# Running sums of a feed-forward's down product: kept in SBUF between loads and stores, or added to in memory by accumulating transfers

## The chip, the cores and the metric

The kernel runs on one core of a Trainium2 chip. The metric is the device time of one execution in microseconds (us), as the median of three runs; the runs lie between 1864.41 and 1867.26 us.

## The reference, cut to what matters

One layer on 256 tokens of width 2048: a mixer (dilated attention and a gated linear attention), a layer norm, a convolved feed-forward of inner width 5632, and a second layer norm. Everything is float32. The change lies in the last lines.

```
ALPHA = (2 * DEPTH) ** 0.25
...
def _conv_ffn(x, w_gate, w_up, conv_w, conv_b, w_down):
    g = x @ w_gate
    ...
    return (jax.nn.silu(gc) * (x @ w_up)) @ w_down
...
        x = _layernorm(ALPHA * x + mix, ln1_g[i], ln1_b[i])
        ffn = _conv_ffn(x, ffn_w_gate[i], ffn_w_up[i], ffn_conv_w[i], ffn_conv_b[i], ffn_w_down[i])
        x = _layernorm(ALPHA * x + ffn, ln2_g[i], ln2_b[i])
```

So the second norm is taken of `ALPHA * x + ffn`, where x is the output of the first norm; `ALPHA * x` is called the residual below.

## The kernel before

**Products.** A float32 product is made of three fast ones: each operand is split into a high part (ScalarE, a rounding copy, tile `whi` for weights) and a low part (VectorE, source minus high part, tile `wlo`), both at lines 145 and 146 (`split`). TensorE then multiplies high by high, high by low and low by high. All weights stream in as pieces of 128x1024 numbers, `raw` or `quarter`, on SyncE's queue. So for nearly every piece of weight there is one ScalarE and one VectorE instruction of over 1 us, then some 5 us of matmuls for four pieces.

**Feed-forward.** The 44 tiles of the inner width are cut into six parts (`FSPLIT = (8, 8, 8, 8, 8, 4)`). In each part the gate and up products of 8 tiles (4 in the last part) are made, convolved and gated into `h`; then `down_group` multiplies `h` with the rows of w_down that belong to the part. The down product of a part has 256 x 2048 sums: four column blocks n of 512, each for two token halves t, so eight blocks of 128x512, in the two PSUM banks of `mbank`. They are to be added up over the six parts.

**Order.** In part p > 0 steps of several kinds are mixed by a string, `MIX`: `u` a step of a Strassen-like unit (`seven`, products named fguA, fguB, fguD, fguE) that makes four tiles of gate and up at once, `t` a gate or up tile made directly (fg, fu), `A` a transposing and gating step of the unit of the part before (matmuls `pt`), `d` a step of the down product of the part before (`wd_t`), `B` an `A` of the last unit. For eight tiles it is `uAtAuAtAdutdudtdutdudtutdtd`, so two `d` finish one n. The framework's scheduler then sets the order of each engine's queue; each engine runs its own queue strictly in that order. A boundary between two parts means below: the last `d` of one string and the first `u A t A u A t A` of the next.

**Running sums before.** Tile `ACC[t][n]` is a block in device memory. In part 0 `more` copies the finished PSUM bank to SBUF with ScalarE (line 1118) and stores it ("spill") from GpSimd's queue. In parts 1 to 4 `ahead` has fetched the block into SBUF one n earlier (tile `af`, GpSimd's queue), `more` adds the PSUM bank to it with VectorE (line 1116) and spills it to a new block. The last four blocks of part 4 (n of 2 and 3) stay in SBUF; its first four are spilled and reloaded from ScalarE's queue into `acc` (line 1213), and part 5 adds its PSUM banks to all eight in SBUF with VectorE.

**Residual before.** x lies transposed in memory, `X1F`, eight blocks `x1f`. In the down product of part 0, after the first `d` of each n, eight float32 matmuls of blocks of x1f with `weighted` (ALPHA times the identity, made by VectorE at the start) add the turned residual to the PSUM banks (line 1137, tile names `wd_t<-weighted,x1f`; the compiler makes two records of each).

**Sums of x.** The units need sums of blocks of x: `sums_get(j)` fetches blocks j and j+4 of X1F into tiles `x1p`, `sums_part(j)` makes the sums (`comb`). These are called by `pump` between the steps of part 0.

**Buffers.** Most tiles of 128x512 (`blk`) in this stage share eight buffers: af, wd, x1p, x1f, and s, u, c of the units. A new tile takes the buffer of one that is done with, and the first instruction that writes it waits for the last reader of the old one, which for a spilled tile is the DMA.

## Time and profile before

| what | value |
| --- | --- |
| median of three runs | 1867.16 us (1864.41 to 1867.26) |
| profiled execution: span, first to last instruction | 1866.8 us |
| what lies around the span of the profiled execution | no time of its own is printed; the median of the runs is 0.4 us above the span |
| TensorE (PE) busy | 1819.1 us, 97% |
| VectorE (DVE) busy | 1442.1 us, 77% |
| ScalarE (ACT) busy | 1084.1 us, 58% |
| GpSimd (POOL) busy | 238.7 us, 13% |
| mean granted TensorE clock | 0.991 |
| feed-forward, from the end of the first norm | 1130 to 1867 us of the span |

An engine's busy time is the sum of its instructions; PEld is the loading of weights into TensorE, beside its matmuls. In a row of the timeline the square bracket tells how long the engine sat idle before the instruction and what released it. The boundaries between parts lie at about 1349, 1481, 1611 and 1740 us of the span (into parts 2, 3, 4 and 5).

### The profile page before, as it was taken

What the parts mean: (1) busy time and instruction counts of PE and PEld (TensorE: products, weight loads), DVE (VectorE), ACT (ScalarE), POOL (GpSimd) and SP (SyncE); (2) the same over time, 40 slices, a digit from 0 to 9 for tenths busy, and PEclk for the clock granted to TensorE, in tenths of its full rate; (3) what the DMA queues carried; (4) which work ended last, traced back from release to release, by engine and by line L of the source; (5) the groups of instructions that cost most, each with busy time, mean ns of one, the idle gap of its engine ahead of it and who ended that gap; (6) DMA issues with size and microseconds to landing.
All of it is one profiled execution on the core that took longest, in us unless ns stands there. A gap on an engine that the chain in (4) does not pass through costs nothing.

```text
span 1866.8 us, 25420 instructions
## 1 busy us (share of the span) xinstructions
PE 1819.1 (97%) x8974; PEld 1523.3 (82%) x8974; DVE 1442.1 (77%) x1715; ACT 1084.1 (58%) x1400; POOL 238.7 (13%) x361
## 2 busy tenths in 40 slices
PE   8999999999999999999999999999999999999896
PEld 6887887888887888888788868888888888888785
DVE  6978899788697978865856556886696877877878
ACT  5656586565666667646645345655565546655553
POOL 0121111111111111211300001011111110110211
PEclk9999999999999999999999999999999999999998
DMA  8898888987979798897965538569679779778782
GB/s 298 280 343 229 279 273 265 337 241 242 339 207 342 204 325 268 267 358 247 329 206 191 169 118 298 182 193 322 214 217 352 221 215 347 206 247 328 191 271 91
DMA packets 145420, 478.54 MB, mean 256 GB/s; under 512 B 17649, under 2 KB 27916, under 8 KB 145292
## 3 DMA queue, kind: packets, MB, share of 16 engines
q1 hardware_dynamic: 96764, 345.09, 51.6%
q0 software_dynamic: 34416, 118.62, 25.6%
q10 hardware_dynamic: 14112, 13.21, 2.2%
q8 instruction: 70, 1.15, 0.2%
q14 instruction: 58, 0.48, 0.1%
HBM read 382.41 MB, written 32.67 MB: 222 GB/s over the span
## 4 chain that ended last, share of the span: by engine, by line
PE 72%; issue 11%; DVE 7%; DMA 6%; ACT 2%; POOL 1%; SPq 0%; ACTq 0%; DVEq 0%; POOLq 0%
PE qk L236 9%; PE qk L238 5%; PE wd_t L273 4%; PE wd_t L272 4%; PE wd_t L274 4%; DMA raw<-in_wp 3%; DVE wlo L146 3%; PE gqk L236 3%; PE fguE L343 3%; PE fu L236 3%; PE fg L236 3%; PE fguA L343 2%; PE mD L343 2%; PE mA L343 2%; PE mE L343 2%
## 5 line engine op out<-in xcount | busy, mean ns | idle before, releaser
L146 DVE TENSOR_TENSOR wlo<-quarter,whi 128x1024 fp32r<-128x1024 f32 x484 | 578.8, 1219 | 217.1 <-issue 58.7
L145 ACT ACTIVATE whi<-quarter 128x1024 fp32r<-128x1024 f32 x484 | 504.8, 1057 | 301.0 <-DVE quarter L356 59.8
L145 ACT ACTIVATE whi<-raw 128x1024 fp32r<-128x1024 f32 (+1 forms) x346 | 358.5, 1051 | 246.8 <-DMA raw<-in_wp 121.6
L146 DVE TENSOR_TENSOR wlo<-raw,whi 128x1024 fp32r<-128x1024 f32 (+1 forms) x346 | 413.2, 1213 | 99.1 <-ACT whi L145 50.3
L236 PE MATMUL qk<-x,whi 128*128 128x512 f32 x768 | 189.2, 397 | 0.0
L359 POOL DMA_DIRECT2D quarter<-quarter x120 | 106.6, 912 | 616.4 <-DVE quarter L356 150.9
L236 PEld LDWEIGHTS qk<-x,whi 128*128 128x128 f32 x768 | 142.9, 188 | 30.2 <-issue 1.4
L356 DVE TENSOR_TENSOR quarter<-quarter,quarter 128x1024 f32<-128x1024 f32 x120 | 142.5, 1216 | 1.7 <-DMA quarter<-in_wp 1.5
L273 PE MATMUL wd_t<-wlo,h 128*128 128x512 f32 x352 | 137.4, 391 | 0.6 <-DVE wlo L146 0.6
L272 PE MATMUL wd_t<-whi,h 128*128 128x512 f32 x352 | 137.4, 393 | 0.2 <-ACT whi L145 0.2
L274 PE MATMUL wd_t<-whi,h 128*128 128x512 f32 x352 | 136.6, 389 | 0.0
L238 PEld LDWEIGHTS qk<-x,wlo 128*128 128x128 f32 x768 | 98.5, 191 | 3.7
L238 PE MATMUL qk<-x,wlo 128*128 128x256 f32 x768 | 99.6, 283 | 0.0
L236 PE MATMUL fu<-x,whi 128*128 128x512 f32 x368 | 87.9, 391 | 0.3 <-DVE gc L1045 0.3
L236 PE MATMUL fg<-x,whi 128*128 128x512 f32 x352 | 84.1, 391 | 0.0
L236 PEld LDWEIGHTS fu<-x,whi 128*128 128x128 f32 x368 | 68.3, 188 | 14.8 <-PE pt L1086 1.1
L274 PEld LDWEIGHTS wd_t<-whi,h 128*128 128x128 f32 x352 | 66.1, 188 | 14.2 <-DVE h L146 0.3
L273 PEld LDWEIGHTS wd_t<-wlo,h 128*128 128x128 f32 x352 | 66.2, 188 | 13.6 <-DVE wlo L146 0.9
L272 PEld LDWEIGHTS wd_t<-whi,h 128*128 128x128 f32 x352 | 65.9, 188 | 13.8 <-ACT whi L145 0.6
L236 PEld LDWEIGHTS fg<-x,whi 128*128 128x128 f32 x352 | 65.5, 188 | 13.3
L236 PE MATMUL gqk<-x,whi 128*128 128x512 f32 x256 | 65.3, 407 | 3.9 <-ACT whi L145 3.9
L236 PEld LDWEIGHTS gqk<-x,whi 128*128 128x128 f32 x256 | 49.5, 198 | 17.3 <-ACT whi L145 7.4
(375 smaller groups left out, 3185.2 us busy)
## 6 DMA issues: line engine op xcount, KB each, us to landing
raw<-in_wp SPq DMA_DIRECT2D x342, 512.0 KB, 6.0
quarter<-in_wp SPq DMA_DIRECT2D x304, 512.0 KB, 7.2
quarter<-quarter POOLq DMA_DIRECT2D x120, 512.0 KB, 10.1
af<-acc POOLq DMA_DIRECT2D x32, 256.0 KB, 6.9
acc<-af POOLq DMA_DIRECT2D x28, 256.0 KB, 5.7
sp<-c POOLq DMA_DIRECT2D x14, 256.0 KB, 9.5
bias<-bvd ACTq DMA_DIRECT2D x32, 96.0 KB, 6.6
v<-vs ACTq DMA_DIRECT2D x24, 128.0 KB, 4.6
```

The lines of the kernel that those rows point to most:

```text
L145: newest[:] = [nc.scalar.activation(hi, src, AF.Copy)]
L146: nc.vector.tensor_tensor(lo, src, hi.bitcast(F32), op=ALU.subtract)
L236: nc.tensor.matmul(ps, parts(kc)[0], opnd(kc), start=(kc == 0), stop=False)
L238: nc.tensor.matmul(ps[:, S:], parts(kc)[1], opnd(kc)[:, :S], start=False, stop=(kc == nk - 1))
L272: nc.tensor.matmul(ps, xh, hi, start=first, stop=False)
L273: nc.tensor.matmul(ps, xh, lo, start=False, stop=False)
L274: nc.tensor.matmul(ps, xl, hi, start=False, stop=last)
L343: nc.tensor.matmul(ps, a(kc)[which], w[:, k * 512 : (k + 1) * 512], start=(first and w is hi and which == 0 and kc == 0), stop=(w is lo an ...
L356: tt(a, a, b, op=ALU.add)
L359: nc.gpsimd.dma_start(a, b, accum_op=ALU.add)
```

## The change

ACC becomes four tiles in memory, one for each n, of 128x2x512. Their first value is the residual: `sums_part(j)`, which already has blocks j and j+4 of x in SBUF, also turns them with plain transposes on TensorE (`pr`, four for a block), ScalarE copies each full bank times ALPHA to a tile `res`, and GpSimd's queue stores it. Then in parts 0 to 4 (in part 4 only for n of 0 and 1) ScalarE copies each finished PSUM bank to a tile `wd`, and a DMA with `accum_op=add` on GpSimd's queue adds it to the block in memory. The fetches of x1f and of af and VectorE's adds of these parts are gone, but for n of 2 and 3 in part 4, which are fetched and added as before. `weighted` and its matmuls are gone.

```
--- before.py
+++ after.py
@@ -419,8 +419,6 @@
 
     ident = cpool.tile([P, P], F32, name="ident")
     make_identity(nc, ident)
-    weighted = cpool.tile([P, P], F32, name="weighted")
-    nc.vector.tensor_scalar(weighted, ident, ALPHA, None, op0=ALU.mult)
     prm = cpool.tile([P, NPAR], F32, name="prm")
     nc.gpsimd.dma_start(prm, par)
     pc = lambda c: prm[:, c : c + 1]
@@ -1093,7 +1091,7 @@
         return seven("fgu", X1, comb1, AT["fgu", f0], keep_it), [turned(f) for f in range(f0, f0 + 4)]
 
     F = [[None] * 4 for _ in range(2)]
-    ACC = [[None] * 4 for _ in range(2)]
+    ACC = [dpool.tile([P, 2, 512], F32, name=f"acc_{n}") for n in range(4)]
 
     def down_group(part, nf, hs):
 
@@ -1103,25 +1101,20 @@
 
         def ahead(n):
 
-            for t in range(2):
-                if part:
-                    st[n, t] = fetch("af", ACC[t][n])
-                else:
-                    st[n, t] = fetch("x1f", X1F[2 * n + t])
+            if part == len(FSPLIT) - 2 and n > 1:
+                for t in range(2):
+                    F[t][n] = fetch("af", ACC[n][:, t])
 
         def more(n, pss):
             for t in range(2):
-                a = F[t][n] if last else st[n, t] if part else blk("wd0")
-                if part:
-                    nc.vector.tensor_tensor(a, a, pss[t], op=ALU.add)
+                if F[t][n] is not None:
+                    nc.vector.tensor_tensor(F[t][n], F[t][n], pss[t], op=ALU.add)
                 else:
+                    a = blk("wd")
                     nc.scalar.activation(a, pss[t], AF.Copy)
+                    nc.gpsimd.dma_start(ACC[n][:, t], a, accum_op=ALU.add)
                 if last:
-                    nc.vector.bn_stats(stats[t][:, n, :], a)
-                elif part == len(FSPLIT) - 2 and n > 1:
-                    F[t][n] = a
-                else:
-                    ACC[t][n] = spill("acc", a)
+                    nc.vector.bn_stats(stats[t][:, n, :], F[t][n])
 
         def step(n, k0):
             def g():
@@ -1131,20 +1124,11 @@
                     if n < 3:
                         ahead(n + 1)
                 chunk_step(st["ps"], hk, nf, at, k0)
-                if not k0 and not part:
-                    for t in range(2):
-                        for k in range(4):
-                            nc.tensor.matmul(
-                                st["ps"][t][:, k * P : (k + 1) * P],
-                                st[n, k // 2][:, (k % 2) * S + t * P : (k % 2) * S + (t + 1) * P],
-                                weighted, start=False, stop=False
-                            )
                 if k0 + 4 == nf:
                     more(n, st["ps"])
             return g
 
         if not last:
-            ahead(0)
             return [step(n, k0) for n in range(4) for k0 in range(0, nf, 4)]
         for n in range(0, 4, 2):
             at = [AT["wd", part] + 2 * (n + i) for i in range(2)]
@@ -1176,7 +1160,19 @@
         return f
 
     def sums_part(j):
-        return lambda: part1(j)
+        def f():
+            part1(j)
+            for h in (j, j + 4):
+                pt = bank("pr")
+                for t in range(2):
+                    for k in range(2):
+                        c = t * S + k * P
+                        nc.tensor.transpose(pt[:, c : c + P], XF[h, t][:, k], ident)
+                a = blk("res")
+                nc.scalar.activation(a, pt, AF.Copy, scale=ALPHA)
+                c = (h % 2) * S
+                nc.gpsimd.dma_start(ACC[h // 2][:, :, c : c + S], a.rearrange("p (t c) -> p t c", t=2))
+        return f
 
     idle = lambda: None
     sums = [sums_get(0), idle, sums_get(1), sums_part(0), idle, sums_get(2), sums_part(1), idle, sums_get(3), sums_part(2), idle, sums_part(3)]
@@ -1210,7 +1206,7 @@
             for n in range(2):
                 for t in range(2):
                     F[t][n] = acc[:, 2 * t + n]
-                    nc.scalar.dma_start(F[t][n], ACC[t][n])
+                    nc.scalar.dma_start(F[t][n], ACC[n][:, t])
         older = down_group(part, nf, [h() for h in hs])
     act_set(ACT_LN_EXP, held_by[0])
     norm = [mean_and_scale(t) for t in range(2)]
```

Where the instructions stand now is shown at three places. The first is **TensorE's** queue. Before, in part 1, the residual stands between the first down step and the unit's third product, as four rows of two matmuls at each of four such places:

```order
L273 MATMUL wd_t_1402_11177<-wlo_11203,h_10192 128x512
L274 MATMUL wd_t_1402_11177<-whi_11202,h_10192 128x512
L1137 MATMUL wd_t_1401_11176<-weighted,x1f_10963 128x128 x2
L1137 MATMUL wd_t_1401_11176<-weighted,x1f_10965 128x128 x2
L1137 MATMUL wd_t_1402_11177<-weighted,x1f_10963 128x128 x2
L1137 MATMUL wd_t_1402_11177<-weighted,x1f_10965 128x128 x2
L343 MATMUL fguB_11234<-whi_11243,comb_1273_10046 128x512 x4
L343 MATMUL fguB_11234<-wlo_11244,comb_1273_10046 128x512 x2
```

After, the same place has no such rows:

```order
L273 MATMUL wd_t_1416_11239<-wlo_11261,h_10194 128x512
L274 MATMUL wd_t_1416_11239<-whi_11260,h_10194 128x512
L343 MATMUL fguB_11284<-whi_11293,comb_1273_10048 128x512 x4
L343 MATMUL fguB_11284<-wlo_11294,comb_1273_10048 128x512 x2
L343 MATMUL fguB_11284<-whi_11303,comb_1273_10048 128x512 x4
```

They are replaced by transposes in part 0, between two gate or up tiles (fu and fg), at four places of two rows:

```order
L238 MATMUL fu_10437<-x_1246_9933,wlo_10434 128x256 x4
L238 MATMUL fu_10437<-x_1247_9934,wlo_10434 128x256 x4
L1170 MATMUL pr_10492<-ident,x1p_10313 128x128 x4
L1170 MATMUL pr_10500<-ident,x1p_10315 128x128 x4
L236 MATMUL fg_10520<-x_1244_9931,whi_10510 128x512 x4
L236 MATMUL fg_10520<-x_1245_9932,whi_10510 128x512 x4
L236 MATMUL fg_10520<-x_1246_9933,whi_10516 128x512 x4
```

So four groups of sixteen records leave the down steps in part 1, and four groups of eight come into part 0, the last of them right before the first unit.

The second is **ScalarE's** queue at the boundary into part 3 (1481 us), with what each instruction waits for in brackets (DMASW is a DMA of GpSimd's queue, DMAHW one of SyncE's or ScalarE's). `s` is the copy of the unit's first product; `gc` behind it starts the gating of the older unit. Before:

```order
L1030 ACTIVATE pa_13200<-fu_13167 128x256 [waits PE_49]
L145 ACTIVATE whi_13319<-raw_13317 128x1024 [waits DMAHW3_49,PE_49]
L145 ACTIVATE h_12345<-gc_13112 128x256 [waits DVE_49]
L145 ACTIVATE whi_13325<-raw_13323 128x1024 [waits DMAHW4_49,PE_49]
L145 ACTIVATE whi_13396<-quarter_13253 128x1024 [waits PE_49,Activation_49]
L145 ACTIVATE whi_13406<-quarter_13255 128x1024 [waits DVE_49,PE_49,Activation_49]
L369 ACTIVATE s_13302<-fguA_13261 128x512 [waits DMASW3_49,DMASW4_49,DVE_49,PE_49]
L1038 ACTIVATE gc_13309<-pt_13304,prm 128x256 [waits PE_49]
L145 ACTIVATE whi_13416<-quarter_13257 128x1024 [waits DVE_49,Activation_49]
L145 ACTIVATE whi_13426<-quarter_13259 128x1024 [waits DVE_49,Activation_49]
```

After:

```order
L1028 ACTIVATE pa_13194<-fu_13161 128x256 [waits PE_49]
L145 ACTIVATE whi_13309<-raw_13307 128x1024 [waits DMAHW3_49,PE_49]
L145 ACTIVATE h_12351<-gc_13106 128x256 [waits DVE_49]
L1114 ACTIVATE wd_13236<-wd_t_1601_13111 128x512 [waits DMASW3_49,PE_49]
L1114 ACTIVATE wd_13239<-wd_t_1602_13112 128x512 [waits DMASW4_49,PE_49]
L145 ACTIVATE whi_13315<-raw_13313 128x1024 [waits DMAHW4_49]
L145 ACTIVATE whi_13386<-quarter_13243 128x1024 [waits PE_49,Activation_49]
L145 ACTIVATE whi_13396<-quarter_13245 128x1024 [waits DVE_49,PE_49,Activation_49]
L145 ACTIVATE whi_13406<-quarter_13247 128x1024 [waits DVE_49,PE_49,Activation_49]
L369 ACTIVATE s_13292<-fguA_13251 128x512 [waits DMASW5_49,PE_49]
L1036 ACTIVATE gc_13299<-pt_13294,prm 128x256 [waits PE_49]
L145 ACTIVATE whi_13416<-quarter_13249 128x1024 [waits DVE_49,Activation_49]
```

Two copies `wd` have come in, and s no longer waits for the spills of the last n (DMASW3 and DMASW4 at the spills acc_13243 and acc_13246 of the next place) but for one older DMA (DMASW5, the accumulating transfer of n = 2, acc_10045<-wd_12960 in the next place).

The third is **GpSimd's** queue at the same boundary. `quarter<-quarter` are accumulating transfers between SBUF tiles that the units use. Before:

```order
L359 DMA quarter_13383<-quarter_13556 128x1024 [waits DMASW1_49,DMAHW3_49,DVE_49,Activation_49]
L359 DMA quarter_13385<-quarter_13558 128x1024 [waits DMAHW4_49,DVE_49,Activation_49]
L112 DMA acc_13243<-af_12836 128x512 [waits DMASW3_49,DVE_49]
L112 DMA acc_13246<-af_12838 128x512 [waits DMASW4_49,DVE_49]
L118 DMA af_13516<-acc_12735 128x512 [waits DMASW4_49]
L359 DMA quarter_13387<-quarter_13560 128x1024 [waits DMAHW5_49,DVE_49,Activation_49]
L359 DMA quarter_13389<-quarter_13562 128x1024 [waits DMASW7_49,DMAHW6_49,DVE_49,Activation_49]
L118 DMA af_13518<-acc_12738 128x512 [waits DMASW0_49,PE_49]
```

After:

```order
L1115 DMA acc_10045<-wd_12960 128x512 [waits DMASW5_49,Activation_49]
L1115 DMA acc_10045<-wd_12963 128x512 [waits DMASW6_49,Activation_49]
L359 DMA quarter_13373<-quarter_13542 128x1024 [waits DMAHW3_49,DMASW7_49,DVE_49]
L1115 DMA acc_10046<-wd_13236 128x512 [waits DMASW0_49,Activation_49]
L1115 DMA acc_10046<-wd_13239 128x512 [waits DMASW1_49,Activation_49]
L359 DMA quarter_13375<-quarter_13544 128x1024 [waits DMAHW4_49,DMASW2_49,DVE_49]
L359 DMA quarter_13377<-quarter_13546 128x1024 [waits DMAHW5_49,DMASW3_49,DVE_49]
L359 DMA quarter_13379<-quarter_13548 128x1024 [waits DMAHW6_49,DMASW4_49,DVE_49]
```

The two fetches af among the unit's transfers are gone; the spills of the last n (acc_13243 and acc_13246) have become accumulating transfers (into acc_10046), which wait for ScalarE where the spills waited for VectorE.

## The prediction

> **What bounds the kernel now.** I read the page first: busy time, then the chain that ended last.
>
> ```profile
> PE 1819.1 (97%) x8974; PEld 1523.3 (82%) x8974; DVE 1442.1 (77%) x1715; ACT 1084.1 (58%) x1400; POOL 238.7 (13%) x361
> PE 72%; issue 11%; DVE 7%; DMA 6%; ACT 2%; POOL 1%; SPq 0%; ACTq 0%; DVEq 0%; POOLq 0%
> ```
>
> TensorE (PE) is busy for 97% of the span and holds 72% of the chain, so a matmul that goes is worth its own length wherever TensorE never waits. Where it does wait I took from the busy times by stretch, cut at the boundaries between parts. The columns are start:end, length, then busy us and count of PE, PEld, DVE, ACT and POOL, granted clock, DMA share, GB/s.
>
> ```profile
> 1212.00:1232.00 20.00, 18.61 (x91) 15.47 (x91) 20.00 (x29) 12.27 (x20) 4.72 (x6) 1.00 0.82 188
> 1232.00:1349.00 117.00, 117.00 (x602) 100.23 (x602) 79.40 (x86) 65.04 (x79) 11.02 (x18) 1.00 0.76 251
> 1349.00:1481.00 132.00, 131.94 (x650) 111.69 (x649) 104.17 (x125) 76.99 (x97) 17.83 (x27) 1.00 0.83 264
> 1481.00:1508.00 27.00, 26.22 (x137) 21.70 (x135) 25.99 (x38) 18.43 (x30) 2.95 (x4) 1.00 0.68 194
> 1611.00:1638.00 27.00, 25.46 (x133) 21.09 (x131) 25.25 (x38) 18.14 (x30) 2.95 (x4) 1.00 0.66 188
> 1740.00:1767.00 27.00, 22.33 (x94) 16.90 (x93) 24.77 (x33) 18.74 (x27) 6.67 (x11) 0.94 0.74 208
> ```
>
> TensorE loses 1.39 us in the first stretch (before part 1), nothing in the second, 0.06 around the boundary into part 2 (1349 us), 0.78 into part 3, 1.54 into part 4 and 4.67 into part 5. In each losing stretch VectorE (DVE) is busy 92 to 100%: there VectorE is the bound, and work taken from it or stalls before it count.
>
> Why do equal boundaries lose 0.06 at 1349 us and 0.78 and 1.54 later? The timelines of ScalarE and VectorE there tell (start, length, engine, line; in brackets the idle time before and what ended it):
>
> ```profile
> 1346.86 1.28 ACT L1118 ACTIVATE wd<-wd_t 128x512 f32<-128x512 f32 x2 [0.67 <-PE wd_t L274]
> 1353.03 0.60 ACT L369 ACTIVATE s<-fguA 128x512 f32<-128x512 f32 x1 [0.51 <-PE fguA L343]
> 1482.81 0.60 ACT L369 ACTIVATE s<-fguA 128x512 f32<-128x512 f32 x1 [3.58 <-DMA acc<-af]
> 1483.89 0.48 DVE L1039 SCALAR_TENSOR_TENSOR gc<-pt,prm,gc 128x255 f32<-128x255 f32 x1 [0.78 <-ACT gc L1038]
> 1613.10 0.60 ACT L369 ACTIVATE s<-fguA 128x512 f32<-128x512 f32 x1 [4.33 <-PE fg L236]
> 1614.19 0.48 DVE L1039 SCALAR_TENSOR_TENSOR gc<-pt,prm,gc 128x255 f32<-128x255 f32 x1 [1.53 <-ACT gc L1038]
> 1743.23 0.60 ACT L369 ACTIVATE s<-fguA 128x512 f32<-128x512 f32 x1 [1.39 <-DMA acc<-af]
> 1744.32 0.94 DVE L1039 SCALAR_TENSOR_TENSOR gc<-pt,prm,gc 128x255 f32<-128x255 f32 x2 [1.38 <-ACT gc L1038]
> ```
>
> In the last three boundaries ScalarE's s stands 3.58, 4.33 and 1.39 us, because its buffer is one that the spills of the last n have still to read out (the middle row names fg, but the queue's waits are the same spills as in the row of 1482.81). Behind s stands gc, and VectorE idles for it: 0.78, 1.53 and 1.38 us. In the first two TensorE's loss is the same 0.78 and 1.54: the stall goes straight through. At 1349 us, where part 0's sums are copied by ScalarE, none of it shows. That boundary is before's own picture of the changed order: two wd copies, no adds, an s that waits 0.51 us.
>
> **The change, part by part.**
>
> *TensorE, residual.* Out go four groups of sixteen records; the chain of waits gives their length, first and last of four. In come 32 transposes; the nearest rows are those of the unit's results.
>
> ```profile
> 1241.62 1.78 PE wd_t L1137 x16
> 1334.70 1.78 PE wd_t L1137 x16
> 1740.90 0.27 PE L1086 MATMUL pt<-ident,c 128*128 128x128 f32 x1
> 1741.01 0.27 PE L1086 MATMUL pt<-ident,u 128*128 128x128 f32 x1
> 1741.69 1.17 PE L343 MATMUL fguD<-whi,comb 128*128 128x512 f32 x4
> ```
>
> Out: 4 x 1.78 = 7.1 us, all in the stretch without idle time. In: 0.11 us from start to start (eight take 0.79 us to the next matmul), 32 x 0.11 = 3.5 us. Net -3.6 us. The transposes need x1p, which is fetched at least two gate or up tiles ahead. A tile's length (chain) and the fetch's landing (DMA issues: count, size, median us to landing):
>
> ```profile
> 1230.62 3.63 PE fu L236 x16
> 1234.24 1.91 PE fu L238 x16
> x1p<-x1s POOLq DMA_DIRECT2D x8, 256.0 KB, 5.9
> ```
>
> Two tiles are 11.1 us against 5.9, and the two banks (`bank`) have no other user in part 0. I charge no wait.
>
> *Before part 1 (1219 us).* Three of the four transpose groups (2.6 us) come before the wait there:
>
> ```profile
> 1219.77 0.73 PE L343 MATMUL fguA<-wlo,x 128*128 128x512 f32 x2 [1.40 <-DVE wlo L146]
> ```
>
> TensorE arrives later while VectorE's work is unchanged, so up to 1.4 us of the new work may hide here; but VectorE itself waits for TensorE's fg and fu in that stretch and moves back with it. Bounds 0 and -1.4; I take the middle, -0.7. ScalarE gets eight res copies of 0.6 us into stretches where it has idle time. The eight stores replace eight fetches of x1f in number.
>
> *VectorE's adds become ScalarE's copies,* 28 of them, with eight already there:
>
> ```profile
> L1116 DVE TENSOR_TENSOR af<-af,wd_t x36: 669/682/689, 1392.9 to 1852.7; 128x512 f32<-128x512 f32 x36
> L1118 ACT ACTIVATE wd<-wd_t x8: 580/599/601, 1259.3 to 1347.5; 128x512 f32<-128x512 f32 x8
> ```
>
> VectorE loses about 5 us a part, ScalarE (busy 58%) gains as much. Away from the boundaries TensorE loses nothing on VectorE today, so I count nothing there. PSUM banks come free by ScalarE; the next n needs them a tile later, over 5 us against two copies of 1.2 us.
>
> *The stall of s.* s now takes the buffer of n = 2, not of the last n. How far apart these are in time, the stores into part 3 show:
>
> ```profile
> 1443.12 0.54 POOL L112 DMA_DIRECT2D acc<-af  x1 [18.92 <-DVE af L1116]
> 1477.36 1.47 POOL L112 DMA_DIRECT2D acc<-af  x2
> DMA to landing us min/median/max: 2.4/5.7/14.9
> ```
>
> The older one is issued some 35 us before s, the longest landing is 14.9 us: the stall goes even for transfers twice as slow. With the loss at 1349 us as the remainder, part 3 gains 0.78 - 0.06 = 0.7 and part 4 gains 1.54 - 0.06 = 1.5 us. The next lateness there is VectorE's own queue, which has also lost its two adds (2 x 0.68 us).
>
> *Into part 5.* Less covers the gating here. VectorE is full but for the 1.38 us idle. Without that wait the chain to the unit's third product is 1.4 us shorter at least; with the two adds gone as well, 2.7 us. I take -2.0. Then the clock: TensorE's longest wait of the stage ends at 1760.53 us, and behind it the granted clock falls.
>
> ```profile
> 1760.53 0.73 PE L343 MATMUL fguB<-wlo,comb 128*128 128x512 f32 x2 [2.91 <-DVE wlo L146]
> 1762.00:1763.00 1.00, 1.00 (x4) 0.81 (x3) 1.00 (x2) 1.00 (x2) 0.00 (x0) 0.50 0.00 0
> ```
>
> The stretch 1740 to 1767 has a mean clock of 0.94: 27 x 0.06 = 1.6 us of clock missing, at 0.50 therefore some 3.2 us long, a loss of 1.6. After the wait of 1.40 us at 1219 us the clock was 1.00 in its stretch. A wait of 2.91 - 2.0 = 0.9 us should cost no clock: -1.6; bounds 0 and -1.6. The Trainium skill, "TensorE: Matmul & The Clock Gate", section "Part 1: The HAM clock gate (the "warmup" mystery)", says that the clock halves after an idle window of about 3.4 us, and that the windows run freely; the trace agrees in the halving, but here a wait of 2.91 us was enough. By the skill's length alone the clock would not have fallen here at all and the sum would be 1.6 us worse.
>
> *Reloads in part 5.* ScalarE's queue itself issues the reloads of the first four blocks and stands until the store, now the accumulating transfer, has landed:
>
> ```profile
> 1777.82 0.35 ACTq L1213 DMA_DIRECT2D acc<-acc  x1
> 1783.32 5.44 PE fguD L343 x24
> 1798.89 1.06 ACT L145 ACTIVATE whi<-quarter 128x1024 fp32r<-128x1024 f32 x1 [1.32 <-DMA acc<-af]
> 1805.08 5.44 PE fguE L343 x24
> ```
>
> Queued behind it are weight copies whi: for the third quarter of fguD (needed at 1783.3 + 2.7 = 1786.0) and of fguE (1807.8). Before, these copies stood right behind the reloads of 1777.8 and 1798.4, so 8 and 9 us were in hand, of which the copy takes 1.1. Price from 0 to 7.4 us (the second rival); I take 0.5.
>
> *DMA.* 36 stores become accumulating, 36 fetches go, eight stores come.
>
> ```profile
> q1 hardware_dynamic: 96764, 345.09, 51.6%
> q0 software_dynamic: 34416, 118.62, 25.6%
> quarter<-quarter POOLq DMA_DIRECT2D x120, 512.0 KB, 10.1
> 1257.00:1800.00 543.00, 535.95 (x2616) 450.73 (x2615) 418.26 (x488) 312.84 (x389) 75.96 (x116) 1.00 0.82 262
> ```
>
> q1 needs 0.516 x 1866.8 / 345.09 = 2.8 ns of all 16 engines per KB (MB of 10^6), so 0.73 us per 256 KB. q0 holds 62.9 MB of accumulating quarter transfers; the other 55.7 MB at q1's rate take 155 us of its 478, which leaves 5.1 ns per KB, 1.34 us per 256 KB. So: -36 x 0.73 + 36 x (1.34 - 0.73) + 8 x 0.73 = +1.5 us of 98 us idle (18% of 543). Nothing, if adding into memory costs what adding into SBUF costs; no row shows the former. The Trainium skill, "DMA: Bandwidth & Descriptors", section "Anatomy of one DMA — SWDGE (gpsimd) path", warns that completion can take surprisingly long when the target is HBM, with a fit of 2.0 us + bytes/436e3; that is an estimate of 2.6 us for 256 KB, by which the reloads cost 0 and the sum is 0.5 better. The median of 5.7 us above is longer, and I keep to it.
>
> *Queues.* GpSimd's in-order queue loses fetches that waited for buffers; the quarter transfers behind get no later. SyncE's order is unchanged. The end after 1840 us keeps its work.
>
> **Sum.** -3.6 - 0.7 - 0.7 - 1.5 - 2.0 - 1.6 + 0.5 = -9.6 us, against a span of 1866.8. The median of the runs is 0.4 above it; 1867.2 - 9.6 = **1857.6 us**.
>
> **Rivals.**
> 1. Only the matmuls count (chance 0.24): ScalarE, with more copies in its queue at the boundaries, becomes late itself, and gc waits as before. For it: two copies stand ahead of s, 1.28 us. Against: ScalarE idled 3.58 and 4.33 us there. 1867.2 - 3.6 = 1863.6.
> 2. The reloads block ScalarE (0.10): if the accumulating transfers land after three times the median, 17.1 us, the reloads come 11.4 us later, whi is ready at 1790.3 and 1810.9, 4.3 and 3.1 us late; +7.4 us instead of 0.5: 1864.5. For it: ScalarE already stood 1.32 us, and the accumulating quarter transfers, twice as large, take 10.1 us. Against: no store took over 14.9.
> 3. Slower (0.08): adding into memory holds the DMA engines. A transfer of x us saves 0.73 + 0.73, so 36 (x - 1.46) must exceed 98: from x = 4.2, three times the 1.34, weights come late and every further us costs 36. At x = 5, 29 us: 1887. Against: the same engines add into SBUF at 1.34.
>
> **How the numbers follow.** My forecast has 0.58. About 0.2% (3.7 us) is what a measurement of this kernel can tell from no change: faster means below 1863.4. The forecast lies there, rivals 1 and 2 straddle it (half of 1, a third of 2), rival 3 is slower. Faster 0.58 + 0.12 + 0.04 = 0.74; slower 0.08 + 0.01 = 0.09; same 0.17. Lower end: all gains at their bounds (3.6 + 1.4 + 0.7 + 1.5 + 2.7 + 1.6 = 11.5, and the rest of part 5's loss, 2.0) give 1853.7; upper end 1866, past rivals 1 and 2, which leaves out rival 3 and some of 2.
>
> **What would show it.** TensorE's records 32 fewer, and the four 1.78 us groups gone; s within 1 us of its product at the three boundaries; the stretches into parts 3, 4 and 5 losing about 0.1, 0.1 and 2.7 us, with clock 1.00; ScalarE idle at most a few us before the reloads' neighbours; DMA share near 0.82. The prediction is wrong if wd copies or s wait longer than 2 us, if wd transfers take over 10 us to land, or if whi waits for raw grow.

## The result, and the profile after

The changed kernel takes 1859.2 us (median of seven runs, 1856.63 to 1864.85) against 1867.16 us of the kernel before on the same chip (seven runs, 1863.83 to 1871.25). The ratio is 0.9955, with a 95% interval of 0.9942 to 0.9967: faster by 8.4 us, give or take 2.3. The prediction said 1857.6 us.

The span of the profiled execution went from 1866.8 to 1854.9 us, which is 11.9 us and not 8. Some 3.7 us of it lie before the feed-forward, where the change takes out nothing but the making of `weighted`. So the spans are not compared below, but the same places in the two traces. First the page, busy time and the chain by engine:

```profile
PE 1809.0 (98%) x8942; PEld 1516.2 (82%) x8942; DVE 1424.3 (77%) x1686; ACT 1101.4 (59%) x1436; POOL 235.6 (13%) x333
PE 79%; DVE 9%; DMA 6%; issue 2%; ACT 2%; POOL 1%; SPq 0%; ACTq 0%; DVEq 0%; POOLq 0%
```

TensorE has 32 records fewer and is busy for ten microseconds less: 3.6 us are the residual, and most of the rest is the granted clock, which between 20 and 1840 us of the span was halved for 20.5 us in the kernel before and for 6.9 us here. VectorE (DVE) lost 18 us and ScalarE (ACT) gained 17. Then busy time by stretch, cut at the boundaries, which now lie 7 to 11 us earlier (start:end, length, busy us and count of PE, PEld, DVE, ACT, POOL, clock, DMA share, GB/s):

```profile
1218.75:1342.00 123.25, 123.25 (x603) 104.56 (x604) 91.38 (x98) 72.83 (x89) 12.95 (x16) 1.00 0.83 250
1345.00:1372.00 27.00, 26.64 (x140) 22.45 (x139) 25.73 (x39) 18.76 (x31) 1.03 (x2) 1.00 0.66 181
1473.80:1500.80 27.00, 26.89 (x142) 22.83 (x141) 26.25 (x39) 19.27 (x31) 1.07 (x2) 1.00 0.66 181
1602.00:1629.00 27.00, 26.32 (x139) 22.17 (x138) 25.41 (x39) 18.44 (x31) 1.20 (x2) 1.00 0.67 180
1729.00:1756.00 27.00, 23.84 (x113) 19.59 (x112) 27.00 (x37) 19.36 (x27) 6.55 (x11) 1.00 0.84 213
1756.00:1789.00 33.00, 32.16 (x140) 25.68 (x140) 24.23 (x22) 19.06 (x22) 8.81 (x11) 1.00 1.03 278
1250.00:1788.00 538.00, 532.84 (x2597) 448.92 (x2596) 403.33 (x463) 327.01 (x419) 68.61 (x83) 1.00 0.85 250
```

TensorE idles 0.36, 0.11, 0.68 and 3.16 us into parts 2, 3, 4 and 5, where the kernel before idled 0.06, 0.78, 1.54 and 4.67. New are 0.84 us in the stretch with the reloads. The DMA share of the whole feed-forward rose from 0.82 to 0.85. Next s at the four boundaries, and the waits of TensorE over 0.2 us from part 1 to the reloads (timelines of ScalarE and of TensorE; in brackets the idle time and what ended it):

```profile
1345.66 0.60 ACT L369 ACTIVATE s<-fguA 128x512 f32<-128x512 f32 x1 [0.46 <-PE fguA L343]
1474.47 0.60 ACT L369 ACTIVATE s<-fguA 128x512 f32<-128x512 f32 x1 [0.46 <-PE fguA L343]
1602.79 0.60 ACT L369 ACTIVATE s<-fguA 128x512 f32<-128x512 f32 x1 [0.46 <-PE fguA L343]
1732.33 0.58 ACT L369 ACTIVATE s<-fguA 128x512 f32<-128x512 f32 x1
```

```profile
1218.74 0.74 PE L343 MATMUL fguA<-wlo,x 128*128 128x512 f32 x2 [1.33 <-DVE wlo L146]
1358.21 3.92 PE L236 MATMUL fu<-x,whi 128*128 128x512 f32 x16 [0.21 <-DVE gc L1043]
1615.66 3.92 PE L236 MATMUL fu<-x,whi 128*128 128x512 f32 x16 [0.52 <-DVE gc L1043]
1748.63 0.73 PE L343 MATMUL fguB<-wlo,comb 128*128 128x512 f32 x2 [3.16 <-DVE wlo L146]
1773.32 1.21 PE L343 MATMUL fguD<-whi,comb 128*128 128x512 f32 x4 [0.80 <-ACT whi L145]
```

s no longer stands for spills anywhere. But the wait at fguB into part 5 is 3.16 us, longer than the 2.91 of before, and there is a wait for whi in fguD of part 5. Last the new pieces: the transposes (count, ns min/median/max, first and last start), the transfers (count, size, median us to landing), and what holds the reload, GpSimd's queue and ScalarE's:

```profile
L1170 PE MATMUL pr<-ident,x1p x32: 272/272/273, 1164.1 to 1212.1; 128*128 128x128 f32 x32
acc<-wd POOLq DMA_DIRECT2D x36, 256.0 KB, 8.3
acc<-res POOLq DMA_DIRECT2D x8, 256.0 KB, 3.7
...
1760.84 0.89 POOL L359 DMA_DIRECT2D quarter<-quarter  x1 [17.73 <-ACT whi L145]
1761.41 2.12 POOL L1115 DMA_DIRECT2D acc<-wd  x2
...
1772.21 2.01 ACT L145 ACTIVATE whi<-quarter 128x1024 fp32r<-128x1024 f32 x2 [9.81 <-PE fguD L343]
```

All 32 transposes lie before 1213 us. The accumulating transfers land after 8.3 us in the median. The one that the first reload waits for is issued at 1761.4 us, behind a quarter transfer for which GpSimd's queue stood; ScalarE idles 9.81 us until it has landed (the bracket names fguD, which was long done; the instruction just ahead is the reload, at 1771.76).

**How long a wait really costs.** The idle time in brackets is less than what a wait takes from TensorE. Two rows of a run without waits (changed kernel) and three rows with one (kernel before, into part 5):

```profile
1782.19 1.07 PE L343 MATMUL fguA<-whi,x 128*128 128x512 f32 x4
1783.10 0.62 PE L343 MATMUL fguA<-wlo,x 128*128 128x512 f32 x2
...
1744.52 1.07 PE L343 MATMUL fguD<-whi,comb 128*128 128x512 f32 x4
1745.74 0.73 PE L272 MATMUL wd_t<-whi,h 128*128 128x512 f32 x2 [0.16 <-ACT whi L145]
1747.22 0.73 PE L343 MATMUL fguD<-wlo,comb 128*128 128x512 f32 x2 [0.75 <-DVE wlo L146]
```

Four matmuls need 0.91 us from start to start, 0.23 each, though a record is longer: neighbouring records overlap. In the lower rows it is 1.48 us from 1745.74 to 1747.22 with two matmuls in between, so 1.02 us are lost, and the bracket shows 0.75. (Two waits for weights in the runs below tell the same in the table's differences: 0.57 us of bracket cost 0.86, and 0.29 cost 0.60.) The four waits of before into part 5 that were shorter than the last (0.16, 0.75, 0.63 and 0.23 us, 1.8 together) so cost some 2.9 us. The Trainium skill, "TensorE: Matmul & The Clock Gate", section "Step-by-step: what each phase is for", says that in a stream the drain of one matmul hides behind the next one's fill, and that a matmul that stands alone pays it. That this is where the 0.27 us go no run here shows.

**Place by place.** Therefore each matmul's start in a trace was subtracted from the same matmul's start in the trace of the kernel before. Inside the parts this difference hardly moves; the table has the change of its median from one quiet stretch to the next. "Ahead of 1" runs from 1150 to 1223 us of the kernel before, "part 0's sums" to 1340, the columns of the parts to the middle of each, "reloads" from 1782 to 1795. Behind it stand the sum, the difference of the medians of the runs on the same chip, and how long the granted clock was halved into part 5.

| kernel | ahead of 1 | part 0's sums | into 2 | into 3 | into 4 | into 5 | reloads | later | sum | medians | clock halved |
| --- | --- | --- | --- | --- | --- | --- | --- | --- | --- | --- | --- |
| changed | +3.5 | -7.2 | +0.5 | -1.2 | -1.1 | -4.4 | +1.7 | 0 | -8.2 | -8.0 | none |
| changed, again | +2.9 | -7.2 | +0.7 | -0.6 | -2.3 | -2.8 | +0.8 | 0 | -8.4 | -6.9 | 3.4 us |
| residual only | +4.0 | -7.2 | -0.3 | +0.8 | -0.6 | -0.2 | 0 | 0 | -3.4 | -4.8 | 6.8 us |
| sums only | +0.9 | 0 | +0.5 | -1.0 | -1.5 | -2.7 | +0.7 | 0 | -3.3 | -5.5 | 3.4 us |
| nine blocks | +0.4 | 0 | -0.3 | 0.0 | -1.5 | -1.5 | 0 | 0 | -3.0 | -2.3 | 3.4 us |
| reloads late | +2.4 | -7.2 | -0.2 | -1.2 | -0.9 | -3.0 | 0 | +0.4 | -9.7 | -9.9 | 3.4 us |
| s on the last | +3.6 | -7.2 | +1.7 | +2.2 | +0.9 | -1.4 | 0 | 0 | -0.2 | +0.6 | 6.8 us |
| d earlier | +2.9 | -7.2 | +0.1 | -0.5 | -1.4 | -2.1 | 0 | -4.9 | -13.0 | -12.4 | none |
| added twice | +5.1 | -7.2 | -0.3 | -1.6 | -1.1 | -4.4 | +2.2 | +1.9 | -5.3 | -5.1 | none |
| plain stores | +2.4 | -7.2 | -0.3 | -0.9 | -1.2 | -2.8 | 0 | 0 | -10.0 | -11.9 | 3.4 us |

The sums agree with the medians within 2.3 us. In the kernel before the clock was halved for 3.4 us into part 5, which costs 1.7 us; a row with "none" has gained that much there by the clock alone. In the two rows with 6.8 us the clock was already halved during the last microsecond of TensorE's wait, and it cost some 1.1 us more than in the kernel before. (In "d earlier" matmuls have changed places across the last columns, so only their sum counts; the kernel "tile first" below is left out, since it turns matmuls round ahead of part 1.)

### The profile page after: what moved, and what is told of

It is laid out like the page before. It is cut to its first block, busy times and chain, and to the rows that moved or that the text cites. A ratio compares the mean times of both kernels' runs of the same rounds, so it can differ in the third digit from the quotient of the medians.

```text
span 1854.9 us, 25320 instructions
## 1 busy us (share of the span) xinstructions
PE 1809.0 (98%) x8942; PEld 1516.2 (82%) x8942; DVE 1424.3 (77%) x1686; ACT 1101.4 (59%) x1436; POOL 235.6 (13%) x333
## 3 DMA queue, kind: packets, MB, share of 16 engines
q0 software_dynamic: 34480, 111.28, 26.5%
## 4 chain that ended last, share of the span: by engine, by line
PE 79%; DVE 9%; DMA 6%; issue 2%; ACT 2%; POOL 1%; SPq 0%; ACTq 0%; DVEq 0%; POOLq 0%
PE qk L236 8%; PE qk L238 4%; DVE wlo L146 4%; PE wd_t L272 4%; PE wd_t L273 4%; PE wd_t L274 4%; PE gqk L236 3%; PE fg L236 3%; PE fguE L343 3%; PE fu L236 3%; PE fguA L343 2%; PE fguD L343 2%; PE mD L343 2%; PE mA L343 2%; PE mE L343 2%
## 5 line engine op out<-in xcount | busy, mean ns | idle before, releaser
L146 DVE TENSOR_TENSOR wlo<-quarter,whi 128x1024 fp32r<-128x1024 f32 x484 | 579.8, 1223 | 230.2 <-issue 55.6
L356 DVE TENSOR_TENSOR quarter<-quarter,quarter 128x1024 f32<-128x1024 f32 x120 | 143.1, 1223 | 1.4 <-DMA quarter<-in_wp 1.2
```

Source lines behind the costliest of these rows:

```text
L146: nc.vector.tensor_tensor(lo, src, hi.bitcast(F32), op=ALU.subtract)
L356: tt(a, a, b, op=ALU.add)
```

## Experiments

Theory: the gain is TensorE's shorter residual, s that no longer stands on the spills, and VectorE's adds that are gone into part 5, less the stand at the reloads. Its main rival: only the matmuls count. Each ratio is to the kernel before, on the same chip; code is cut to the lines that tell.

**Residual only** (e1). The kernel before, its adds kept; the residual is stored by transposes into FIRST, and part 0's copies are added to it in memory:

```
-                else:
-                    st[n, t] = fetch("x1f", X1F[2 * n + t])
...
+                elif part:
                     ACC[t][n] = spill("acc", a)
+                else:
+                    ACC[t][n] = FIRST[n][:, t]
+                    nc.gpsimd.dma_start(ACC[t][n], a, accum_op=ALU.add)
```

> The residual part alone: first value by transposes, part 0's ScalarE copies added to it in memory by eight accumulating transfers; the adds of parts 1 to 4 stay on VectorE with their fetches and spills, as in the kernel before. Theory (the two parts of the change work in different places and add up): part 0 becomes 7.1 us shorter (four groups of matmuls go), the stretch ahead of part 1 becomes 3.5 us longer (32 transposes, none of them hidden by the wait of 1.3 us there, since VectorE moves back with TensorE), s still stands 3 to 4 us into parts 3 and 4, and TensorE loses 0.8, 1.5 and 4.7 us into parts 3, 4 and 5 as before. Sum -3.6 us, ratio 0.998. Rival 1 (only matmuls count; the whole measured gain is here): -8 us, ratio 0.9955. Rival 2 (the wait ahead of part 1 hides 0.7 us or more of the transposes): -4.3 us, and the wait at the matmuls of wlo is 0.7 us shorter.

Measured: 0.9973 (0.9960 to 0.9986), -5.0 us; by the places -3.4. The four groups give -7.2, and the stretch with the transposes costs 4.0: the wait ahead of part 1 hides none of them in this run, against rival 2 of the expectation. s and TensorE at the third boundary are as in the kernel before (ScalarE's and TensorE's timeline):

```profile
1477.83 0.60 ACT L369 ACTIVATE s<-fguA 128x512 f32<-128x512 f32 x1 [3.79 <-DMA acc<-af]
1482.53 0.33 PE L1084 MATMUL pt<-ident,c 128*128 128x128 f32 x1 [0.45 <-DVE gc L1043]
```

So the residual carries about half of the gain, not the whole: rival 1 of the expectation (0.9955) lies just outside the interval, and the trace has no gain into parts 3 and 4. Into part 5 s does not stand in this run, though the spills and adds there are those of the kernel before: their transfers had landed in time. What s costs there so varies from run to run. The +0.8 into part 3 is a wait for weights in the middle of the part (0.29 us of idle time at 1537.8), which the profiled execution of before happened not to have.

**Sums only** (e2). The changed kernel with the matmuls of the residual back in part 0, and part 0's copies stored plainly as the first value:

```
+                    if part:
                         nc.gpsimd.dma_start(ACC[n][:, t], a, accum_op=ALU.add)
+                    else:
+                        nc.gpsimd.dma_start(ACC[n][:, t], a)
```

> The running sums alone: ScalarE's copies and accumulating transfers in parts 1 to 4, but the residual stays in the matmuls of part 0, whose copies are stored plainly as the first value. Theory: the four groups of 1.78 us and the fetches of x1f stay, so part 0 is as before; s stands under 1 us; TensorE loses 0.1, 0.7 and 3.2 us into parts 3, 4 and 5 in place of 0.8, 1.5 and 4.7, and 1.2 to 1.6 us at the reloads in part 5, where ScalarE's queue stands some 10 us for the accumulating transfer. Sum -1.5 to -4.5 us (the upper end if the clock also stays whole in part 5), ratio 0.9976 to 0.9992. Rival (only matmuls count): 0, ratio 1.000, with VectorE waiting for ScalarE's gc into parts 3 and 4 as before.

Measured: 0.9970 (0.9958 to 0.9981), -5.6 us; by the places -3.3, which lies in the range expected (-1.5 to -4.5), as the ratio alone does not. Into parts 3, 4 and 5 it gains 1.0, 1.5 and 2.7 us, and s stands nowhere:

```profile
1481.75 0.60 ACT L369 ACTIVATE s<-fguA 128x512 f32<-128x512 f32 x1 [0.46 <-PE fguA L343]
```

The rival (no gain without the matmuls) falls. Do the two halves add up? By places they give -3.4 and -3.3, with 1.1 us of clock lost in the first that the kernel before did not lose: -7.8 without it. The changed kernel has -8.2 and -8.4, and -6.5 and -8.4 without the 1.7 us that the clock gave its first profile. So they add up within the scatter of one profile, some 1 to 2 us.

**Nine blocks** (e3). The kernel before with one buffer more, so that s takes one that was spilled an n earlier; nothing else of the sums changes:

```
-    now[:] = ctx.enter_context(tc.tile_pool(name="last", bufs=1)), (8, 9, 1)
+    now[:] = ctx.enter_context(tc.tile_pool(name="last", bufs=1)), (9, 7, 1)
```

> The kernel before with nine buffers of 128x512 in the feed-forward in place of eight (and seven of 128x256 in place of nine, to make room), so that s takes a buffer that was stored one n earlier. All of VectorE's adds, fetches and spills stay. Theory (the stall of s on the last spills goes straight through to TensorE): s stands under 1 us into parts 3, 4 and 5, VectorE no longer idles ahead of gc, TensorE loses 0.1 to 0.3 us into parts 3 and 4 in place of 0.8 and 1.5, and up to 1.4 us less into part 5: -1.8 to -3.3 us, ratio 0.9982 to 0.9990. Rival (VectorE's own two adds set the loss, s has slack): TensorE loses the same 0.8 and 1.5 us with s early, ratio 1.000. Fewer small buffers could cost something: then pa, gc or comb wait for a buffer, and the stretches ahead of part 1 or in the boundaries lose more.

Measured: 0.9990 (0.9978 to 1.0003), so by time alone not told from no change. The trace tells it. ScalarE now waits for the product and not for the spills, and TensorE idles 0.38 us in place of 0.78 and of 1.54 (timeline; busy time by stretch, as above):

```profile
1483.56 0.60 ACT L369 ACTIVATE s<-fguA 128x512 f32<-128x512 f32 x1 [2.07 <-PE fguA L343]
1482.00:1509.00 27.00, 26.62 (x141) 22.50 (x140) 26.71 (x39) 18.32 (x29) 2.89 (x4) 1.00 0.70 203
1612.00:1639.00 27.00, 26.62 (x141) 22.48 (x140) 26.71 (x39) 18.80 (x30) 2.90 (x4) 1.00 0.69 200
```

Places: -1.5 into part 4 and -1.5 into part 5. Into part 3 it is 0.0, because a wait for weights at 1544 us (0.57 us of idle time) takes back what the boundary had won. With VectorE's adds all in place, s alone is worth these. Sums only has 1.2 us more into part 5; VectorE's two adds, which are gone there, take 1.28.

**s on the last** (e5). The other way round: the changed kernel, but s is written into the buffer of the last ScalarE copy of the n before:

```
-            st["s"] = blk("s")
+            st["s"] = last_wd[0] if name == "fgu" and last_wd else blk("s")
```

> The changed kernel with the stall of s put back and nothing else: into parts 2 to 5 s is written into the buffer of the last ScalarE copy of the n before (n of 3, t of 1), so that it waits until that accumulating transfer has landed. ScalarE's copies, the adds in memory and the residual are as in the changed kernel. By its trace that transfer is issued 3.7 us before s is ready and lands a median of 8.3 us later. Theory (s standing in ScalarE's queue holds back gc, so VectorE, so TensorE): s stands 4 to 7 us, VectorE idles for gc 1 to 4 us and TensorE loses as much more into each of parts 2 to 5: +4 to +12 us over the changed kernel, ratio to the kernel before 0.998 to 1.002. Rival (the adds' removal from VectorE made the gain; a late s is covered): same as the changed kernel, 0.9955.

Measured: 1.0006 (0.9994 to 1.0018). That is 9.5 us more than the changed kernel (0.9955), and all of its gain is gone. Not all of the 9.5 us is the stall itself: the mean granted clock of these twelve runs is 0.9895, against 0.9920 in the seven of the changed kernel, by which some 4.7 us (0.0025 of 1866, an estimate) are lost clock. In the trace the clock was halved for 3.5 us behind the wait into part 3, which is 1.7 of the +2.2 there. Into part 4, from ScalarE through VectorE to TensorE (three timelines; s bears the name of the buffer, wd):

```profile
1610.42 0.60 ACT L370 ACTIVATE wd<-fguA 128x512 f32<-128x512 f32 x1 [4.72 <-DMA acc<-wd]
1611.51 0.48 DVE L1038 SCALAR_TENSOR_TENSOR gc<-pt,prm,gc 128x255 f32<-128x255 f32 x1 [3.58 <-ACT gc L1037]
1615.04 0.33 PE L1085 MATMUL pt<-ident,c 128*128 128x128 f32 x1 [2.92 <-DVE gc L1044]
```

One wait, handed on twice: 4.72, 3.58, 2.92. Into parts 2 and 3 s stood 3.63 and 3.75 us and TensorE 1.80 and 1.92: what s stands beyond 1.8 us, TensorE loses. Into part 5, where the last copy is that of n = 1, s stood only 0.32 us, and TensorE reaches the end of its last wait there 2.4 us sooner than in the kernel before, nearly as in the changed kernel (2.7). This and nine blocks show the stall of s as the cause from both sides.

**Reloads late** (e4). The four reloads behind later weight copies in ScalarE's queue:

```
+                    with tc.issue_after(copies[(4, 6)[n]].ins):
                         nc.scalar.dma_start(F[t][n], ACC[n][:, t])
```

> The changed kernel with the four reloads of part 5 later in ScalarE's queue, behind the weight copies of the fifth and seventh step of part 4's down product, by which time the accumulating transfers have landed. Theory (the reload's stand of 9.8 us in ScalarE's queue makes weight copies late and costs TensorE 1.2 to 1.6 us at fguD of part 5): no stand over 3 us at the reloads, no wait of fguD for whi, 1.2 to 1.6 us less than the changed kernel: ratio to the kernel before 0.9946. Rival (the lateness only moves to the next wait in part 5, or the reloads now come too late for the last adds): same time as the changed kernel, ratio 0.9955, or slower by what the last adds wait for acc.

Measured: 0.9952 (0.9936 to 0.9968); by time alone the same as the changed kernel. In the trace the loss at the reloads is gone, and 0.45 us come back later, where an add of VectorE stands behind a late weight (busy time by stretch; TensorE's timeline):

```profile
1762.00:1795.00 33.00, 33.00 (x147) 27.31 (x147) 24.04 (x22) 21.38 (x24) 8.81 (x12) 1.00 1.02 274
1808.01 0.47 PE L272 MATMUL wd_t<-whi,h 128*128 128x512 f32 x1 [0.45 <-DVE af L1111]
```

So the stand of ScalarE's queue is what the 0.8 to 1.7 us at the reloads are.

**Added twice** (e7). Every accumulating transfer issued a second time, into memory that nobody reads:

```
                     nc.gpsimd.dma_start(ACC[n][:, t], a, accum_op=ALU.add)
+                    nc.gpsimd.dma_start(TWICE[n][:, t], a, accum_op=ALU.add)
```

> The changed kernel with each of the 36 accumulating transfers issued twice, the second time into a block of memory that nobody reads. Theory (a transfer takes some 1.7 us of all 16 DMA engines, 36 more are 61 us of the some 80 us in which they idle; they hold nobody as long as weights stay ahead): 0 to +3 us over the changed kernel, from weights a little later (whi waiting for raw) and a longer stand at the reloads if these wait for both; ratio 0.9955 to 0.997. Rival (adding into memory holds the DMA engines, and there is no room left): +15 us and more, weights late in every part, ratio over 1.003.

Measured: 0.9970 (0.9961 to 0.9980), 2.8 us more than the changed kernel. Page rows (queue, packets, MB, share of 16 engines; transfers) and TensorE's timeline:

```profile
q0 software_dynamic: 39664, 120.72, 28.8%
acc<-wd POOLq DMA_DIRECT2D x36, 256.0 KB, 10.8
1670.18 0.50 PE L273 MATMUL wd_t<-wlo,h 128*128 128x512 f32 x1 [0.76 <-DVE wlo L146]
1813.65 0.47 PE L272 MATMUL wd_t<-whi,h 128*128 128x512 f32 x1 [1.94 <-DVE af L1113]
```

q0 had 26.5% of 1854.9 us and has 28.8% of 1864.0: 45 us for 36 transfers, 1.26 us of all 16 engines each. None of the boundaries into parts 2 to 4 pays for it. What it costs are the reloads (+2.2) and weights at two places: at 1670.18 us, in the middle of part 4, TensorE waits for a low part behind copies for which ScalarE had waited 10.60 and 2.74 us for raw (some 1.2 us, part of the column "into 4"), and at 1813.65 us an add of VectorE stands behind a weight for which ScalarE had waited 4.04 us. So even with twice the amount most weights come in time, and a transfer costs far less than the 4.2 us from which rival 3 of the prediction starts: it falls.

**Plain stores** (e8). The adding in memory left out:

```
-                    nc.gpsimd.dma_start(ACC[n][:, t], a, accum_op=ALU.add)
+                    nc.gpsimd.dma_start(ACC[n][:, t], a)
```

> The changed kernel with plain stores in place of the 36 accumulating transfers, of the same blocks from the same queue: the adding into memory is left out. Theory (adding costs little: it is hidden but at the reloads): transfers land in 5 to 6 us in place of 8.3 and the reloads' stand is 2 to 3 us shorter, TensorE's wait for whi in part 5 (1.2 to 1.7 us with its echoes) shrinks or goes, everything else as in the changed kernel: 0 to -2 us, ratio 0.9945 to 0.9955. Rival (adding into memory slows the weights all through the parts): -3 us and more, ratio under 0.994.

Measured: 0.9943 (0.9923 to 0.9963), which by time is not told from the changed kernel. In the trace (page; ScalarE's timeline behind the first reload):

```profile
q0 software_dynamic: 32176, 111.28, 24.6%
acc<-wd POOLq DMA_DIRECT2D x36, 256.0 KB, 5.6
1768.32 1.06 ACT L145 ACTIVATE whi<-quarter 128x1024 fp32r<-128x1024 f32 x1 [6.42 <-DMA acc<-wd]
```

The same blocks land after 5.6 us in place of 8.3, ScalarE stands 6.42 in place of 9.81, and TensorE loses nothing at the reloads. So the price of adding is 2.7 us of landing, which matters at that one place. In the engines' time it is 26.5% of 1854.9 us against 24.6% of 1852.7, 36 us or 0.99 a transfer more than a plain store.

**d earlier** (e6). The better version: late reloads, and in part 5 a second down step ahead of the unit's third product, where TensorE waited 3.16 us for VectorE:

```
-MIX = {8: "uAtAuAtAdutdudtdutdudtutdtd", 4: "uAAuAAdudududududdBdBBB"}
+MIX = {8: "uAtAuAtAdutdudtdutdudtutdtd", 4: "uAAuAAddudududududBdBBB"}
```

> The changed kernel with the late reloads and with one more step of the down product ahead of the unit's third product in part 5 (the string of the last part begins uAAuAAddu in place of uAAuAAdu, and has one d less further on). Theory (into part 5 VectorE is the bound, 27 of 27 us busy, and TensorE's wait of 3.2 us for wlo of fguB is VectorE's arrears; a down step is 5.5 us of TensorE with half of VectorE's work): the wait of 3.2 us goes, and with it the fall of the clock behind it (3.4 us at half speed, 1.7 us), which the kernels with a wait of 2.9 to 3.2 us there all showed but one: -3.2 to -4.9 us against the changed kernel with late reloads alone, ratio to the kernel before 0.9925 to 0.9940. Rival (the arrears only move to fguE or fguD, where the string now has one down step less): the wait appears 10 to 30 us later, ratio 0.995.

Measured: 0.9934 (0.9921 to 0.9948), 1856.37 us. TensorE has no wait left from the boundary to the reloads (busy time by stretch):

```profile
1738.00:1770.00 32.00, 32.00 (x150) 26.37 (x149) 31.13 (x40) 22.98 (x33) 7.37 (x13) 1.00 1.02 282
```

The places give 7.0 us into and through part 5, against 2.6 of reloads late: 4.4 more, the wait and the clock. Of the arrears some 0.8 us turn up later: at 1822.19 us TensorE waits 1.28 us for VectorE's gc, where the changed kernel waits 0.48; the 7.0 us have that in them. By the runs it is 3.9 us below the changed kernel's first ratio, and the two intervals overlap a little; by its ratio it is the best of these kernels.

**Tile first** (e9). d earlier, and in part 1 a gate tile ahead of the unit's first product:

```
-            for kind in MIX[nf]:
+            for kind in MIX[nf] if part > 1 else "tu" * 2 + MIX[nf][8:]:
```

> The kernel with the late reloads and the earlier down step, and in part 1 the first two pairs of the string turned round, so that a plain gate tile stands ahead of the first product of the unit (fguA). Theory (ahead of part 1 VectorE is the bound with the sums of x, and TensorE's wait of 0.7 to 1.8 us for wlo of fguA is arrears, as into part 5): the wait goes, -0.7 to -1.3 us against the kernel without this, ratio 0.9925 to 0.993; the 32 transposes are then paid whole, 3.5 us. Rival (VectorE's arrears follow to fguD): same time, 0.9934.

Measured: 0.9944 (0.9929 to 0.9960): no better. A new wait takes the place of the old one, for a PSUM bank that a copy `res` has still to read:

```profile
1222.60 5.51 PE L236 MATMUL fg<-x,whi 128*128 128x512 f32 x16 [2.18 <-ACT res L1172]
```

Behind it the granted clock is halved for 3.5 us (0.50 from 1222.9 to 1226.3 us). From 1150 to 1345 us this kernel loses 3.6 us to d earlier by the places. Neither the theory nor the rival had this one.

**The changed kernel again** (e10), unchanged.

> The changed kernel once more, unchanged, beside the best one on the same chip. Theory (whether the clock falls behind the wait of 3.2 us into part 5 is not set by the change: it fell in seven of nine profiles with a wait of 2.9 to 3.5 us there): more likely than not the clock now falls for 3.4 us there, and TensorE loses 1.7 us more than in the first profile; wait at fguB 3.2 us, stand at the reloads 8 to 10 us and 1 to 2 us lost there as before. Rival (the change keeps the clock whole): no fall there. The ratio 0.9955 is expected either way.

Measured: 0.9951 (0.9935 to 0.9967). The wait at fguB is 3.16 us in both profiles of this kernel, and behind it the clock is whole in one and halved in the other (busy time by stretch, first profile, then this one twice):

```profile
1749.00:1752.00 3.00, 3.00 (x15) 2.44 (x14) 3.00 (x4) 3.00 (x4) 0.00 (x0) 1.00 0.13 51
...
1750.00:1753.00 3.00, 3.00 (x8) 2.38 (x8) 3.00 (x3) 3.00 (x4) 0.00 (x0) 0.51 0.08 33
1730.20:1757.20 27.00, 23.84 (x107) 19.42 (x106) 27.00 (x37) 19.66 (x27) 6.45 (x11) 0.94 0.82 215
```

Fifteen matmuls in three microseconds, or eight. Over all runs beside it the mean granted clock is the same, 0.9927 in six of the changed kernel and in eleven of the kernel before.

## Why the prediction was right, and where it was not

| step of the prediction | said | shown |
| --- | --- | --- |
| residual on TensorE | -3.6 | -3.7 (-7.2 and +3.5) |
| wait ahead of part 1 hides some | -0.7 | 0 in this trace; -0.4 in the mean of eight traces, within their scatter |
| s into part 3, part 4 | -0.7, -1.5 | -1.2 and -0.6, -1.1 and -2.3 (two profiles) |
| waits into part 5 | -2.0 | -2.7 |
| clock into part 5 | -1.6 | not from the change: -1.7 in the first profile, 0 in the second |
| reloads | +0.5 | +1.7 and +0.8 |
| weights and queues | 0 | +0.5 and +0.7 into part 2 |
| sum | -9.6 | -8.2 (1.7 of it the clock) and -8.4 by places, -8.4 by the ratio |

The mechanism was right: the residual is worth the difference of its matmuls, and s, with the two adds into part 5, the boundaries. The boundary into part 2 in the trace of before was a fair picture of what the others would become. Rival 1 (only matmuls) fell with sums only, nine blocks and s on the last, rival 3 (adding holds the engines) with added twice. That the sum came so near is in part luck: the clock, the reloads and the weights into part 2 came out worse than said, the waits into part 5 better. The steps that failed, in order of size:

*The clock (-1.6).* The step was "a wait of 2.91 - 2.0 = 0.9 us should cost no clock". The last wait did not shrink. What went are the four shorter waits ahead of it; TensorE then reaches fguB earlier, VectorE is busy 27.00 of 27 us, and the wait for its wlo is 3.16 us. VectorE's chain to this wlo is 2.7 us shorter, but TensorE's own way there is 3.0 us shorter, so that VectorE's arrears were gathered at the last of five waits and not removed. Of nine profiles with a wait of 2.9 to 3.5 us there, beside that of the kernel before, seven show a halved clock and the first profile of the changed kernel and added twice do not. So the first profile looked as if the term had been right. The Trainium skill, "TensorE: Matmul & The Clock Gate", section "Part 1: The HAM clock gate (the "warmup" mystery)", says that the windows run freely, and that the point of transition depends on where in a window the first matmul lands; the two profiles of one kernel with the same wait agree with that.

*The reloads (+0.5).* The bounds (0 to 7.4) held the result, the choice was too low. I took the landing from the plain stores, 5.7 us, and the issue as immediate. The transfer lands after some 10 us, and it is issued two microseconds after its copy, because GpSimd's queue stood for a quarter transfer ahead of it. Rival 2 had the mechanism right and the size too large.

*Waits into part 5 (-2.0, shown -2.7).* The bounds were 1.4 (VectorE's wait for gc) and 2.7 (with its two adds), and the upper one holds. The matmul of fguB that waits for wlo starts at 1748.63 us in place of 1760.53, 11.90 earlier, of which 9.17 were there by the middle of part 4: 2.73, and the same in all six profiles in which s does not stand and the adds are gone. Nine blocks, without the adds' part, has 1.50, and residual only, where s happened not to stand, 1.25. So the 2.7 hold against the trace of before; against a run of that kernel in which the spills land in time only some 1.5 us would be left.

*Into parts 3 and 4 (-0.7 and -1.5).* These were counted as idle time in brackets, and each wait costs some 0.27 us more: into part 3 three waits of 0.78 us in all went, and 1.2 us were gained. Into part 4 0.68 us of idle time stayed where 0.1 was expected.

*Ahead of part 1 (-0.7).* All four groups of transposes come before the wait, not three, and it is still 1.33 us (1.40 before): VectorE, which waits for TensorE's fg and fu, moved back with it, as the bound at 0 had it. In the eight traces of the table with transposes this wait is anything from none to 1.83 us, with the same instructions ahead of it, and the place costs 2.4 to 5.1 us, so half a microsecond cannot be told here.

*Into part 2 (+0.5).* Nothing was charged. ScalarE's weight copy there waits for its raw weights, and gc stands behind it (ScalarE's timeline):

```profile
1356.02 1.06 ACT L145 ACTIVATE whi<-raw 128x1024 fp32r<-128x1024 f32 x1 [1.36 <-DMA raw<-in_wp]
```

Plain stores lose nothing there. That more accumulating traffic made these weights late is likely, but late reloads and added twice lose nothing there either, so it stays open.

*DMA.* Estimated were 1.34 us of 16 engines for a transfer; added twice shows 1.26. By the plain stores it is 0.99 more than a store, which with the prediction's 0.73 for one would be 1.7; so between 1.3 and 1.7, and the share came out at 0.85, where 0.82 was expected.

*The signs that were named.* At the boundaries s waits 0.46 us at most, and wd copies 1.0 us. The transfers wd land after 8.3 us in the median, but the longest took 15.1, over the 10 us that were named, and it was such a landing that the reload stood for. ScalarE's waits of whi for raw grew too, from 76.7 us to 88.7 in all from 1150 us on; in this trace TensorE paid for that only into part 2, if at all.

All seven runs lie in the range of 1853.7 to 1866.0 us.

## What to carry to other kernels

Before counting a removed add or store by its own time, look for which instruction took its buffer: here the largest part of what moving the sums saved came from one copy that no longer stood behind a store, and by the trace (not by time alone) one more buffer saves most of it. Where several waits for the same late engine follow each other, removing the first ones can gather the arrears at the last; here other work for the waiting engine at that place, one down step placed earlier, took most of them away. Compare two traces place by place from the starts of the same instructions, since whole spans differ by several microseconds of clock that the change has nothing to do with.

## What the runs showed of the hardware

- A wait takes some 0.27 us more from a stream of 128x512 matmuls than its idle time in the timeline (1.02 against 0.75 us; 0.86 against 0.57 in nine blocks, 0.60 against 0.29 in residual only).
- The clock is halved for 3.4 us or for twice that, also where nothing changed: about 147 us none, 3.4 or 6.8 us, about 1112 us 6.8 or 10.2 us. By 1126 to 1150 us the ten traces above lie between 5.0 us ahead of the kernel before and 3.5 us behind it.
- A wait of TensorE that was followed by a halved clock could be as short as 1.92 us (s on the last, into part 3) or 2.18 us (tile first); one of 2.92 us (s on the last, into part 4) and two of 3.16 and 3.17 us were not followed by one.
- Adding 256 KB into memory by a transfer from SBUF costs 1.26 us of the 16 engines by added twice, some 1.7 by the plain stores, and lands 2.7 us later than a plain store (8.3 against 5.6 us); doubled in number, the transfers land after 10.8 us.
